# Routed experts' blocks add to two DRAM sums by turns instead of one

## The chip, the cores and the metric

The program runs on one core of a Trainium2 chip. The time is the device time of one execution in microseconds, given as the median of three runs. A profile of one execution shows when each engine worked: TensorE (PE, with its weight loads PEld apart), VectorE (DVE), ScalarE (ACT), GpSimd (POOL), and the queues from which transfers are issued (SP's, ACT's and POOL's).

## The reference

One layer: two token mixers, then a mixture of experts on 1024 tokens of width 1024. Only the second half bears on the change:

```
scores = sigmoid(xt @ router)                  # 64 experts, 8 chosen for every token
...
def expert_block(acc, blk):                    # 128 rows of one expert
    toks, wr, e = blk
    xb = x_pad[toks]
    hid = silu(xb @ w1[e]) * (xb @ w3[e])
    return acc.at[toks].add((hid @ w2[e]) * wr[:, None])
...
shared = (silu(xt @ ws1) * (xt @ ws3)) @ ws2
x = x + g2 * (acc[:n_tok] + shared)            # then the last norm
```

## The kernel before, in words

All products are made exact by splitting each fp32 operand into a high and a low part (`wh`, `wl` of weights, `xh`, `xl` of tokens), so one product takes three matmuls.

Ahead of the experts a projection stage turns the merged branches into the residual stream. It reads `mgd`, a DRAM tensor whose 16 parts POOL writes (L802) while TensorE still works on them, through SP's loads at L745, each waiting for `mgd`'s part. In the same stage a tile of zeros is made by POOL (L848) and written once by ACT's queue below the rows of the sum (L849), for rows of padding. The shared expert's output is then written into the sum `acc`, a DRAM tensor of 1024 + 128 rows (L979).

The routed experts (`moe`, L1535) run as a list of blocks of 128 rows, built on the chip: 95 blocks always, with further ones only if the list is longer. The list has two lanes, so that blocks b and b + 2 may share an expert. A block's weights are three pieces of 1 MB, loaded by SP (L1576) two blocks ahead; a piece is skipped where block b - 2 had the same expert. For block b, in the order written by hand in `group` (L1680 to L1706): POOL gathers the token rows of block b + 2 out of `h2d` into `xg`, which has two buffers (L1593); TensorE multiplies block b by the first two matrices (`up`, result `pa`); ACT scales the result of block b - 2 into `y`, which has two buffers (L1669), and POOL adds `y` to the rows of `acc` by an indirect transfer that reads, adds and writes (L1670); ACT and DVE split the weights of coming blocks (L1581, L1586); TensorE transposes the tokens of block b + 1 (`x_t`, L1603, result `pt`), then multiplies block b - 1 by its third matrix (`down`, result `py`). In what follows, "store" is the transfer at L1670 and "gather" the one at L1593. POOL's queue runs them in order, gather of b + 2, store of b - 2, gather of b + 3, and so on.

Each store adds to the tensor that the store before it adds to, so the framework makes POOL wait until the one before has landed.

The last stage (`final`, L1743) loads `acc` and the residual stream `x1d` in the order of rows, two transfers of 64 rows for each tile of 128 (L1740, on SP's queue), multiplies by the gate `g2` (L1777), adds the residual (on TensorE for tiles 0, 1, 3, 4, 6, on DVE at L1782 for the others), and norms and writes the output (L1789, L1790). All loads stand ahead of all output transfers on SP.

Of the kernel before, what the change touches and what calls it, by code (L numbers as in the profile page):

```python
# [10 lines left out]
F32 = mybir.dt.float32  # L11
# [28 lines left out]
def tile_kernel(ctx: ExitStack, tc: tile.TileContext, A: dict, dbg=None):  # L40
# [24 lines left out]
    acc = dram("acc", (T + P, D))  # L65
# [16 lines left out]
    def rsqrt(v, q):  # L82
        """1 / sqrt(v + EPS): the root's reciprocal, then one step of Newton's."""
        y, t = [q.tile([P, 4], F32, name=n, bufs=2)[:, : v.shape[1]] for n in ("rs_y", "rs_t")]
        S.activation(y, v, AF.Sqrt, bias=eps)
        V.reciprocal(y, y)
        V.scalar_tensor_tensor(t, v, EPS, y, ALU.add, ALU.mult)
        V.scalar_tensor_tensor(t, t, -0.5, y, ALU.mult, ALU.mult)
        V.scalar_tensor_tensor(y, t, 1.5, y, ALU.add, ALU.mult)
        return y  # L90
# [9 lines left out]
    def half(dt=F32):  # L100
        """Half of a row of x, or of the low part of h, which takes its place."""
        return hp.tile([P, 512], dt, name="xl", bufs=2 * KD)
# [60 lines left out]
    with tc.manual_schedule(), tc.tile_pool(name="stp", bufs=1, space=PSUM) as qp, ExitStack() as small:  # L163
# [5 lines left out]
        def load_wa(g, which=range(4)):  # L169
            # in the places of weights that come later  # L170
# [31 lines left out]
        # sums over partitions run in four column groups of the array at a time, and sel adds them up  # L202
# [50 lines left out]
        def stats(r):  # L253
            """One over the root of the mean square of each token, over all partitions."""
# [46 lines left out]
        def u_half(m, n, ps):  # L301
            for c in range(4):
                # token = ((c8, j), row); chunk of eight = row * 8 + c8
                dst = us[m][:, :, 32:160].rearrange("p j (r c) -> p c j r", c=8)[:, n * 4 + c]
                V.tensor_copy(dst, ps.rearrange("p (c j r) -> p c j r", c=4, j=8)[:, c])
# [101 lines left out]
    def values(h):  # L407
        """The values of a pair of heads, tokens in rows."""
# [27 lines left out]
    ones_b = ones[:, 0:1].broadcast_to([P, LC])  # L436
    with tc.tile_pool(name="gl", bufs=4, reuse_waits="tile") as q, \
# [9 lines left out]
        def keys(h, d, out):  # L447
            """Decays and keys of a head in one direction, and what the scores take of them."""
# [16 lines left out]
            # all that one table of functions serves, then all of the other's  # L465
# [17 lines left out]
            # the context's keys  # L483
# [48 lines left out]
        def attend(h, d, K, nK):  # L532
            """The head's output in one direction."""
# [15 lines left out]
            for n in order:  # L549
                ki, qi, qin, kp, d3, _ = K[n]  # L550
                # scores of 128 tokens: both chunks on the diagonal, then the block between them
# [68 lines left out]
        def finish():  # L620
            """The normed output, features in rows."""
# [43 lines left out]
    def gates(m):  # L665
        """The sigmoids of both branches' gates, for the features of tile m."""
# [29 lines left out]
    with tc.tile_pool(name="gl2", bufs=1, reuse_waits="tile") as q:  # L696
# [10 lines left out]
        def cmv(t):  # L707
            # (l, (row, c8)) read in the order of the tokens, (c8, l, row)
# [43 lines left out]
    with tc.tile_pool(name="mw", bufs=1, reuse_waits="tile") as qm, \  # L752
            tc.tile_pool(name="mgp", bufs=2, space=PSUM, reuse_waits="tile") as qp:
        wacc = qm.tile([P, D], F32, name="wacc")
        def mod_row(m):
            """Half of the sums behind a later modulation row; the row itself after the second."""
# [71 lines left out]
    def slot(tag, dt=F32R, n=D):  # L828
        """A tile in the place of one that this stage no longer needs."""
        return q.tile([P, n], dt, name=tag, tag=tag)  # L830

    with tc.tile_pool(name="woz", bufs=6, space=PSUM, reuse_waits="tile") as zp, \
# [16 lines left out]
        nc.scalar.dma_start(acc[T : T + P], zr)  # L849
# [8 lines left out]
        def proj(ts):  # L858
            """Sums of the projection's products for these tiles, eight features' tiles deep."""
# [11 lines left out]
        def norm2(t):  # L871
            """Residual, second norm, and the transposed halves of its result."""
# [26 lines left out]
        def scores(n):  # L899
            """The router's scores of half the tokens."""  # L900
# [18 lines left out]
        def shared_up(zp, n, m):  # L919
            """The shared expert's hidden features of tile m for half the tokens."""  # L920
# [37 lines left out]
    with tc.tile_pool(name="shz", bufs=4, space=PSUM, reuse_waits="tile") as zp:  # L958
# [8 lines left out]
        for t in range(8):  # L967
# [11 lines left out]
            nc.sync.dma_start(acc[ts], yo)  # L979
    xs_.close()  # L980
    if stop_after <= 6:
        dump("x1d", x1d)
        dump("h2d", h2d)
        dump("acc", acc)
# [7 lines left out]
    moe(nc, tc, A, ident, h2d, acc, gi, si, beb, iot, meta, lambda: final_load(nc, A, fin, x1d, modr))  # L992
    final(nc, tc, ident, fin, x1d, acc, A["out"])


def s5_main(nc, sp, pp, A, ud, kd, wtd, cad, phd, r8d, yd):
# [5 lines left out]
    for hh in range(2):  # L1002
# [5 lines left out]
        for d in range(2):  # L1008
# [18 lines left out]
            # out of the rotating frame, scan, and back  # L1027
# [56 lines left out]
def s5_tables(nc, tc, A, cad, phd, r8d, more, q, qt, par, bt, ct):  # L1084
# [3 lines left out]
    class Later:  # L1088
        """Keeps the calls of an engine for a chain of steps."""
# [9 lines left out]
    def chain():  # L1099
        """The calls kept so far, one at a time."""  # L1100
# [9 lines left out]
    def weave(*chains):  # L1110
        """Chains that don't wait for each other, by turns."""
# [30 lines left out]
    # sine and cosine of th: quarter turns taken off, then series  # L1142
# [36 lines left out]
    # cos - 1 without cancellation where no quarter turn came off  # L1179
# [4 lines left out]
    # exp(x) - 1: series near zero, the table elsewhere  # L1184
# [32 lines left out]
    def cmul_steps(or_, oi, ar_, ai, br, bi, shp, E=V, own=None):  # L1217
        """(or_ + i oi) = (ar_ + i ai)(br + i bi)."""
# [31 lines left out]
    # powers 0..8 of the decay, upwards and downwards  # L1250
# [18 lines left out]
    # the decay over eight tokens: modulus kept apart from the unit phase  # L1269
# [13 lines left out]
    # output matrices, the imaginary parts with the other sign  # L1283
# [7 lines left out]
    def phases(d, X):  # L1291
        """Unit phases of 0..159 groups of eight tokens."""
# [31 lines left out]
def s5_tables2(nc, tc, last, lastL, A, ident, kd, wtd, qp, q, qt, cmul, phases, bb, ca, pw, dn):  # L1324
    V, S, G, PE = nc.vector, nc.scalar, nc.gpsimd, nc.tensor
    # input matrices, transposed for the tensor engine
# [16 lines left out]
    if True:  # L1343
        # the kernel within eight tokens
        for b8 in range(2):
            kts = q.tile([P, 2560], F32, name=f"big{b8}")[:16, :1920].rearrange("c (g t) -> c g t", g=8)
            kv_ = kts.rearrange("c (i two) t -> c i two t", two=2)
            # each pair of a direction and a group's half in its own columns of the array
# [19 lines left out]
def dispatch(nc, tc, A, ident, ones, sc, gi, si, beb, iot, meta, h2d):  # L1368
    V, S, G, PE = nc.vector, nc.scalar, nc.gpsimd, nc.tensor
    with tc.tile_pool(name="ds", bufs=1, side="right", reuse_waits="tile") as q, \  # L1370
# [17 lines left out]
        # the two largest of every group, by merging sorted pairs  # L1388
# [17 lines left out]
        # a group's rank: how many are larger, or equal and before it  # L1406
# [20 lines left out]
        # weights  # L1427
# [8 lines left out]
        # places: tokens before this one with the same expert  # L1436
# [15 lines left out]
        # blocks of every expert  # L1452
# [17 lines left out]
        # number of blocks, and half of it rounded up: the list's two lanes  # L1470
# [21 lines left out]
        # the expert of every block  # L1492
# [23 lines left out]
        for i in range(0, 64, 4):  # L1516
            # rows and blocks of four choices at a time, the token's number carried by the block's side
# [17 lines left out]
def moe(nc, tc, A, ident, h2d, acc, gi, si, beb, iot, meta, later):  # L1535
    V, S, G, PE = nc.vector, nc.scalar, nc.gpsimd, nc.tensor
    with tc.tile_pool(name="mo", bufs=1, reuse_waits="tile") as q, tc.tile_pool(name="mop", bufs=1, space=PSUM, reuse_waits="tile") as qp:
# [16 lines left out]
        # in the order in which the stage before leaves its memory  # L1554
# [51 lines left out]
        def x_split(b):  # L1606
# [9 lines left out]
            # the token's weight for this block's expert  # L1616
# [49 lines left out]
        def store(b):  # L1666
            if b in YP:
                y = rot(q, [P, D], F32, "y", 2)
                S.mul(y, YP.pop(b), rw[:, b : b + 1])  # L1669
                G.indirect_dma_start(acc, IndirectOffsetOnAxis(ap=si[:, b : b + 1], axis=0), y, None,  # L1670
                                     compute_op=ALU.add)

        def group(lo, hi):
# [6 lines left out]
            for b in range(lo, hi):  # L1680
# [9 lines left out]
                if last:  # L1690
                    # no other block may follow
# [36 lines left out]
def final_load(nc, A, fin, x1d, modr):  # L1728
    """What the last stage needs and the experts' stage leaves room for."""
# [6 lines left out]
def by_row(nc, dst, src, t):  # L1736
    """Rows of 64 columns each, two to a tile, out of the order by columns."""
# [5 lines left out]
def final(nc, tc, ident, fin, x1d, acc, out):  # L1743
    V, S, G, PE = nc.vector, nc.scalar, nc.gpsimd, nc.tensor
    g2, fg = fin[:2]
    with tc.tile_pool(name="fi", bufs=1, reuse_waits="tile") as q, \
            tc.tile_pool(name="fip", bufs=4, space=PSUM, reuse_waits="tile") as qp:
        # the first memory that the experts' stage leaves
        n = len(fin) - 2
        xs = fin[2:] + [q.tile([P, D], F32, name=f"xx{t}") for t in range(n, 8)]  # L1750
        as_ = [q.tile([P, D], F32, name=f"a{t}") for t in range(8)]
        mh = q.tile([P, 1], F32, name="mh")
# [6 lines left out]
        def add(t, x, first):  # L1759
            """Adds x to the sum of a tile on the tensor engine."""  # L1760
# [5 lines left out]
        with tc.manual_schedule():  # L1766
            for t in range(-2, 8):
# [3 lines left out]
                if t >= 0:  # L1771
                    by_row(nc, as_[t], acc[0:T], t)
            for t in on_pe[:4]:
                add(t, xs[t], True)
            for t in range(10):
                if t < 8:
                    V.tensor_tensor(as_[t], as_[t], g2, ALU.mult)  # L1777
# [18 lines left out]
def prep(I):  # L1796
# [32 lines left out]
    # (kind, dir, pair, two, p) -> (two p), kind, (dir pair)  # L1829
# [20 lines left out]
    # constants of the shapes  # L1850
# [37 lines left out]
```

## Time and profile before

| What | Value |
|---|---|
| median of 3 runs | 2209.92 us (2206.99 to 2211.71) |
| span of the profiled execution, which is its own time | 2210.6 us |
| mean granted TensorE clock | 0.967 |
| busy: PE, DVE, ACT, POOL | 2055.3, 1548.2, 1216.4, 526.6 us |
| experts' stage: first token transpose to last `down` | 1174 to 2152 us |
| last stage: first load of the sum to the end | 2170.6 to 2210.6 us |

Busy time says which engine had instructions under way, not which one set the pace; matmuls overlap, so PE looks busier than it is. For the pace one looks at what ended each wait, stage by stage.

### The profile page before, as it was taken

The numbers are of one execution on the slowest core, as the hardware profiler recorded it, in microseconds if no ns is written. First come the engines' busy times: TensorE is split into PE (matmuls) and PEld (weight loads), VectorE is DVE, ScalarE is ACT, GpSimd is POOL, SyncE is SP. The second block draws the span as 40 slices with busy tenths as digits, with TensorE's granted clock in tenths as the row PEclk, the third lists the DMA queues.
The fourth block names the chain that finished last, engine by engine and source line by source line (L and its number), as shares of the span: only waits on it lengthen the run. The fifth ranks groups of instructions, "written<-read, shape, count | busy, mean of one in ns | idle before, by whom it ended". The sixth has DMA issues, their size and how long they took to land.

```text
span 2210.6 us, 28581 instructions
## 1 busy us (share of the span) xinstructions
PE 2055.3 (93%) x10575; PEld 1663.9 (75%) x10575; DVE 1548.2 (70%) x2168; ACT 1216.4 (55%) x1481; POOL 526.6 (24%) x386
## 2 busy tenths in 40 slices
PE   6799999999999999999999999999999998899994
PEld 2488888898777788877777877777777777677771
DVE  7855654744776643345688988988788887888874
ACT  4335543634533311122337887887787787777871
POOL 5510000000011000001003433344353333333342
PEclk7799999999999999999989999999999999999997
DMA  8150101111153543365327999888888889997968
GB/s 300 71 156 20 39 30 39 38 40 38 42 195 113 171 133 116 95 205 206 136 82 270 301 310 307 266 262 239 248 259 259 253 240 339 314 322 231 328 144 210
DMA packets 105210, 407.15 MB, mean 184 GB/s; under 512 B 14850, under 2 KB 21634, under 8 KB 85092
## 3 DMA queue, kind: packets, MB, share of 16 engines
q1 hardware_dynamic: 61408, 255.83, 33.2%
q0 software_dynamic: 34080, 130.93, 22.6%
q10 hardware_dynamic: 9572, 18.46, 2.3%
q8 instruction: 85, 1.39, 0.3%
q14 instruction: 65, 0.53, 0.1%
HBM read 461.24 MB, written 85.48 MB: 247 GB/s over the span
## 4 chain that ended last, share of the span: by engine, by line
PE 42%; DMA 32%; DVE 13%; ACT 5%; issue 5%; POOL 1%; SPq 1%; POOLq 0%; ACTq 0%; DVEq 0%
DMA acc<-y,si 24%; PE z L78 8%; PE z L79 8%; PE z L80 8%; DMA xg<-h2d,gi 3%; DVE wl L1586 3%; PE pa L1623 1%; PE pa L1624 1%; PE pa L1622 1%; ACT wh L1581 1%; PE pt L1603 1%; PE psc L555 1%; DVE xl L1614 1%; PE py L1622 1%; PE py L1623 1%
## 5 line engine op out<-in xcount | busy, mean ns | idle before, releaser
L1586 DVE TENSOR_TENSOR wl<-raw,wh 128x2048 fp32r<-128x2048 f32 x285 | 648.7, 2287 | 99.3 <-ACT wh L1581 99.2
L1581 ACT CAST wh<-raw 128x2048 fp32r<-128x2048 f32 x285 | 535.9, 1916 | 8.3 <-DMA raw<-in_wm_dram 8.3
L1670 POOL DMA_INDIRECT acc<-y,si x95 | 219.4, 2309 | 547.2 <-DMA acc<-y,si 245.9
L1622 PE MATMUL pa<-wh,xh 128*128 128x512 f32 x760 | 304.4, 401 | 0.2 <-ACT xh L1613 0.2
L1623 PE MATMUL pa<-wl,xh 128*128 128x512 f32 x760 | 298.0, 392 | 3.2 <-DVE wl L1586 3.2
L1624 PE MATMUL pa<-wh,xl 128*128 128x512 f32 x760 | 297.3, 391 | 0.1
L79 PE MATMUL z<-xl,wH 128*128 128x512 f32 x672 | 271.0, 403 | 9.0 <-DVE xl L291 9.0
L78 PE MATMUL z<-hH,wH 128*128 128x512 f32 x672 | 268.8, 400 | 2.7 <-ACT hH L288 1.6
L80 PE MATMUL z<-hH,wL 128*128 128x512 f32 x672 | 267.0, 397 | 0.0
L1593 POOL DMA_INDIRECT xg<-h2d,gi x97 | 162.5, 1675 | 91.6 <-issue 48.0
L1669 ACT ACTIVATE y<-py,rw 128x1024 f32<-128x1024 f32 x95 | 106.6, 1122 | 119.8 <-DMA acc<-y,si 119.5
L1623 PEld LDWEIGHTS pa<-wl,xh 128*128 128x128 f32 x760 | 143.0, 188 | 34.9 <-DVE wl L1586 7.9
L1624 PEld LDWEIGHTS pa<-wh,xl 128*128 128x128 f32 x760 | 142.7, 188 | 31.4 <-DVE xl L1614 1.6
L1622 PE MATMUL py<-wh,hh 128*128 128x512 f32 x380 | 163.3, 430 | 1.5 <-ACT y L1669 1.5
L1622 PEld LDWEIGHTS pa<-wh,xh 128*128 128x128 f32 x760 | 142.8, 188 | 27.1 <-ACT xh L1613 0.5
L123 DVE TENSOR_TENSOR wL<-wraw,wH 128x1024 fp32r<-128x1024 f32 x56 | 73.7, 1324 | 124.7 <-ACT wH L118 124.6
L1603 PE MATMUL pt<-ident,xg 128*128 128x128 f32 x760 | 105.9, 285 | 55.7 <-DMA xg<-h2d,gi 55.7
L79 PEld LDWEIGHTS z<-xl,wH 128*128 128x128 f32 x672 | 127.7, 190 | 35.5 <-DVE xl L291 12.5
L1623 PE MATMUL py<-wl,hh 128*128 128x512 f32 x380 | 154.3, 406 | 0.0
L1624 PE MATMUL py<-wh,hl 128*128 128x512 f32 x380 | 154.1, 405 | 0.0
L78 PEld LDWEIGHTS z<-hH,wH 128*128 128x128 f32 x672 | 127.6, 190 | 28.1 <-ACT hH L288 1.8
L1603 PEld LDWEIGHTS pt<-ident,xg 128*128 128x128 f32 x760 | 90.5, 146 | 76.8 <-DMA xg<-h2d,gi 68.5
(520 smaller groups left out, 3863.5 us busy)
## 6 DMA issues: line engine op xcount, KB each, us to landing
raw<-in_wm_dram SPq DMA_DIRECT2D x285, 1024.0 KB
wraw<-in_wz_dram SPq DMA_DIRECT2D x50, 512.0 KB
wk<-in_w_ada_dram SPq DMA_DIRECT2D x64, 256.0 KB
raw<-in_wm_dram POOLq DMA_DIRECT2D x6, 1024.0 KB, 7.4
xl<-in_xcT_dram SPq DMA_DIRECT2D x16, 256.0 KB
mgd<-ga POOLq DMA_DIRECT2D x16, 256.0 KB, 3.1
xr<-in_xc_dram SPq DMA_DIRECT2D x8, 512.0 KB
x1d<-xr ACTq DMA_DIRECT2D x8, 512.0 KB
```

The source lines that it names most:

```text
L78: PE.matmul(out, lh, rh, start=start, stop=False)
L79: PE.matmul(out, lh, rl, start=False, stop=False)
L80: return PE.matmul(out, ll, rh, start=False, stop=stop)
L1581: S.copy(WH[b, c], raw[b % 2][c])
L1586: V.tensor_tensor(WL[b, c], raw[b % 2][c], WH[b, c].bitcast(F32), ALU.subtract)
L1593: G.indirect_dma_start(XG[b], None, h2d, IndirectOffsetOnAxis(ap=gi[:, b : b + 1], axis=0))
L1603: PE.transpose(PX[b][hf][:, k * P : k * P + P], XG[b][:, (hf * 4 + k) * P : (hf * 4 + k + 1) * P], ident)
L1622: PE.matmul(out, lh, rh, start=start, stop=False)
L1623: PE.matmul(out, lh, rl, start=False, stop=False)
L1624: PE.matmul(out, ll, rh, start=False, stop=stop)
L1669: S.mul(y, YP.pop(b), rw[:, b : b + 1])
L1670: G.indirect_dma_start(acc, IndirectOffsetOnAxis(ap=si[:, b : b + 1], axis=0), y, None, compute_op=ALU.add)
```

## The change

There are two DRAM sums. `accs[0]` begins as the shared expert's output, as before; `accs[1]` begins at zero, written by nine transfers of POOL's queue out of the tile of zeros. Even blocks add to the first, odd ones to the second. The last stage loads both and adds them on DVE. (Comments that the change deletes are left out below; they move line numbers alone.)

```diff
-    acc = dram("acc", (T + P, D))
+    accs = [dram(f"acc{i}", (T + P, D)) for i in range(2)]
...
         G.memset(zr, 0.0)
-        nc.scalar.dma_start(acc[T : T + P], zr)
+        nc.scalar.dma_start(accs[0][T : T + P], zr)
+        for t in range(9):
+            nc.gpsimd.dma_start(accs[1][t * P : t * P + P], zr)
...
-            nc.sync.dma_start(acc[ts], yo)
+            nc.sync.dma_start(accs[0][ts], yo)
...
-                G.indirect_dma_start(acc, IndirectOffsetOnAxis(ap=si[:, b : b + 1], axis=0), y, None,
+                G.indirect_dma_start(accs[b % 2], IndirectOffsetOnAxis(ap=si[:, b : b + 1], axis=0), y, None,
                                      compute_op=ALU.add)
...
         as_ = [q.tile([P, D], F32, name=f"a{t}") for t in range(8)]
+        bs_ = [q.tile([P, D], F32, name=f"b{t}") for t in range(8)]
...
                 if t >= 0:
-                    by_row(nc, as_[t], acc[0:T], t)
+                    by_row(nc, bs_[t], accs[1][0:T], t)
+                    by_row(nc, as_[t], accs[0][0:T], t)
...
                 if t < 8:
+                    V.tensor_tensor(as_[t], as_[t], bs_[t], ALU.add)
                     V.tensor_tensor(as_[t], as_[t], g2, ALU.mult)
```

On POOL, at the beginning of the projection stage, the rows before are these (`x` is the tile of zeros, `ga` a finished part of the merged branches):

```order
L802 DMA mgd<-ga 128x4x128 x14
L848 MEMSET x_8153 128x1024
L802 DMA mgd<-ga 128x4x128 x2
L884 TENSOR_SCALAR ss<-ss 128x1
L885 TENSOR_TENSOR ss<-ss,mhalf 128x1
```

And after the change:

```order
L802 DMA mgd<-ga 128x4x128 x14
L848 MEMSET x_8153 128x1024
L852 DMA acc<-x_8153 128x1024 x4
L802 DMA mgd<-ga 128x4x128
L852 DMA acc<-x_8153 128x1024 x3
L802 DMA mgd<-ga 128x4x128
L852 DMA acc<-x_8153 128x1024 x2
L887 TENSOR_SCALAR ss<-ss 128x1
```

Four of the nine zero writes now stand ahead of the last-but-one write of `mgd`, seven ahead of the last. In the experts' stage the rows of POOL stand as before.

On SP, in the last stage, the rows before (`a` takes the sum, `xx` the residual):

```order
L1740 DMA xx_19063<-x1d 64x1024 x2
L1740 DMA a_19066<-acc 64x1024 x2
L1740 DMA a_19067<-acc 64x1024 x2
L1740 DMA a_19068<-acc 64x1024 x2
```

And after (`b` takes the second sum):

```order
L1744 DMA xx_19072<-x1d 64x1024 x2
L1744 DMA b_19083<-acc 64x1024 x2
L1744 DMA a_19075<-acc 64x1024 x2
L1744 DMA b_19084<-acc 64x1024 x2
L1744 DMA a_19076<-acc 64x1024 x2
L1744 DMA b_19085<-acc 64x1024 x2
L1744 DMA a_19077<-acc 64x1024 x2
```

Each of the eight tiles has two more loads, ahead of its old ones, and the outputs still stand behind all loads.

## Rows read from the trace of the kernel before

**Rows 1.** The page's chain that ended last, share of span by line.

```profile
DMA acc<-y,si 24%; PE z L78 8%; PE z L79 8%; PE z L80 8%; DMA xg<-h2d,gi 3%; DVE wl L1586 3%; PE pa L1623 1%; PE pa L1624 1%; PE pa L1622 1%; ACT wh L1581 1%; PE pt L1603 1%; PE psc L555 1%; DVE xl L1614 1%; PE py L1622 1%; PE py L1623 1%
```

**Rows 2.** Chain of waits, 1380 to 1480: start us, us, what.

```profile
1401.23 12.71 DMA acc<-y,si
...
1414.71 9.88 DMA acc<-y,si
```

**Rows 3.** What reads or writes `acc`, whole run: who waited (us, times); landing.

```profile
  POOL acc L1670: 245.9, 34
  ACT y L1669: 119.5, 54
...
DMA to landing us min/median/max: 6.0/9.4/14.6
```

**Rows 4.** POOL in order of time: start us, us, what, [idle before].

```profile
1225.75 2.05 POOL L1670 DMA_INDIRECT acc<-y,si  x1 [1.09 <-DMA acc<-y,si]
```

**Rows 5.** All engines in order of time, the end of the stores.

```profile
2151.66 0.39 PE L1624 MATMUL py<-wh,hl 128*128 128x512 f32 x1
2154.01 1.11 ACT L1669 ACTIVATE y<-py,rw 128x1024 f32<-128x1024 f32 x1 [5.04 <-DMA acc<-y,si]
...
2162.05 1.55 POOL L1670 DMA_INDIRECT acc<-y,si  x1 [5.81 <-DMA acc<-y,si]
```

**Rows 6.** PE in order of time, two token transposes running on.

```profile
1246.79 1.03 PE L1603 MATMUL pt<-ident,xg 128*128 128x128 f32 x8
...
1256.10 1.03 PE L1603 MATMUL pt<-ident,xg 128*128 128x128 f32 x8
```

**Rows 7.** PE in order of time, one that waits.

```profile
1348.29 1.09 PE L1603 MATMUL pt<-ident,xg 128*128 128x128 f32 x8 [3.65 <-DMA xg<-h2d,gi]
```

**Rows 8.** Stretches: L1603's PE, PEld busy (count), clock, DMA share, GB/s.

```profile
1174.00:1300.00 126.00, 14.40 (x112) 12.83 (x111) 1.00 0.90 287
1300.00:1500.00 200.00, 21.29 (x160) 18.03 (x160) 0.99 0.88 281
1500.00:1650.00 150.00, 16.84 (x112) 13.97 (x112) 0.97 0.88 253
1650.00:1800.00 150.00, 16.60 (x116) 14.43 (x117) 0.98 0.81 241
1800.00:2008.00 208.00, 22.08 (x152) 18.35 (x151) 0.95 0.94 315
2008.00:2152.00 144.00, 14.62 (x112) 12.64 (x111) 0.99 0.81 231
```

**Rows 9.** Groups by line, 1174 to 2152: busy, mean ns | idle before.

```profile
L1603 PE MATMUL pt<-ident,xg 128*128 128x128 f32 x760 | 105.9, 285 | 55.7 <-DMA xg<-h2d,gi 55.7
```

**Rows 10.** DMA queues, 1190 to 2160: packets, MB, share of 16 engines.

```profile
q1 hardware_dynamic: 22240, 158.35, 44.3%
q0 software_dynamic: 27035, 101.57, 42.7%
```

**Rows 11.** DMA queues, 2174 to 2192.

```profile
q1 hardware_dynamic: 1303, 4.26, 103.9%
```

**Rows 12.** All engines in order of time, last stage.

```profile
2180.79 5.98 SPq L1740 DMA_DIRECT2D a<-acc  x6
...
2187.47 16.94 SPq L1790 DMA_DIRECT2D out_dram<-a  x8
...
2190.80 1.23 DVE L1777 TENSOR_TENSOR a<-a,fin 128x1024 f32<-128x1024 f32 x1 [1.05 <-DMA a<-acc]
```

**Rows 13.** POOL in order of time, projection stage.

```profile
961.15 0.96 POOL L848 MEMSET x<- 128x1024 f32 x1 [17.10 <-PE z L80]
968.35 0.75 POOL L802 DMA_DIRECT2D mgd<-ga  x1 [6.24 <-DVE ga L801]
```

**Rows 14.** Stretches: PE, PEld, DVE, ACT, POOL busy, clock, DMA share, GB/s.

```profile
970.00:980.00 10.00, 5.75 (x23) 3.12 (x21) 5.11 (x6) 2.34 (x3) 0.75 (x1) 1.00 0.85 296
980.00:990.00 10.00, 8.88 (x32) 6.69 (x33) 3.59 (x3) 3.05 (x4) 0.00 (x0) 0.83 0.96 353
```

More of the change, by code (lines that the diff above doesn't have):

```diff
@@ L983, in tile_kernel @@
         dump("h2d", h2d)
-        dump("acc", acc)
+        dump("acc", accs[0])
         dump("sc", sc)
@@ L991, in tile_kernel @@
         return
-    moe(nc, tc, A, ident, h2d, acc, gi, si, beb, iot, meta, lambda: final_load(nc, A, fin, x1d, modr))
-    final(nc, tc, ident, fin, x1d, acc, A["out"])
+    moe(nc, tc, A, ident, h2d, accs, gi, si, beb, iot, meta, lambda: final_load(nc, A, fin, x1d, modr))
+    final(nc, tc, ident, fin, x1d, accs, A["out"])
 def s5_main(nc, sp, pp, A, ud, kd, wtd, cad, phd, r8d, yd):
@@ L1532, in dispatch, with moe @@
         V.tensor_tensor(si, t1, iv, ALU.add)
-def moe(nc, tc, A, ident, h2d, acc, gi, si, beb, iot, meta, later):
+def moe(nc, tc, A, ident, h2d, accs, gi, si, beb, iot, meta, later):
     V, S, G, PE = nc.vector, nc.scalar, nc.gpsimd, nc.tensor
@@ L1740, in by_row, with final @@
         nc.sync.dma_start(dst[r * 64 : r * 64 + 64], v[t * 2 + r])
-def final(nc, tc, ident, fin, x1d, acc, out):
+def final(nc, tc, ident, fin, x1d, accs, out):
     V, S, G, PE = nc.vector, nc.scalar, nc.gpsimd, nc.tensor
```

## The prediction

> **What bounds the kernel now.** I read the chain that ended last first. Nearly a quarter of the whole span in it is one thing: the landing of the experts' stores into `acc` [rows 1]. All of these lie between 1174 and 2170 us, so in that stage the stores hold about half of the time. The chain in order of time shows how: a store begins at 1401.23, lands 12.71 us later, at 1413.94, and the next begins at 1414.71; so 0.77 us lie between one landing and the next store [rows 2]. A store takes 6.0 to 14.6 us to land, 9.4 in the middle, and both POOL and ACT wait for it (245.9 us and, for a free `y` buffer, 119.5 us) [rows 3]. That the chain binds nearly throughout follows from two starts: the first store that waited for one before it starts at 1225.75 [rows 4], the last one at 2162.05 [rows 5]. Between them lie 91 steps in 936.3 us, 10.29 us each: the middle landing of 9.4 and 0.77, and little else.
>
> TensorE can do better. Where nothing holds it, two token transposes, which come once a block, start at 1246.79 and 1256.10: 9.31 us a block [rows 6]. What holds it is the gather, which stands behind the waiting store in POOL's queue: at 1348.29 a transpose waited 3.65 us for its rows [rows 7], and all such waits sum to 55.7 us over 95 blocks (760 transposes, eight a block) [rows 9]. The stage from 1174 to 2152 is 978 us; 95 blocks at 9.31 are 884. So something under 94 us is lost, 56 in waits, and part of the rest at a lower granted clock, 0.95 to 0.99 in the stretches with waits against 1.00 in the first [rows 8].
>
> Last I asked what stands behind the stores: the DMA engines. Their packets fill 44.3 + 42.7 = 87% of 970 us, the second queue being that of gathers and stores [rows 10]. By stretch the share is 0.81 to 0.94 [rows 8].
>
> **The change in the experts' stage.** No instruction is removed there. A store now waits for the one two blocks before. At 9.31 us a block that one was issued some 18.6 us earlier, more than the longest landing, 14.6 [rows 3]; so neither POOL nor ACT should wait for a landing, the gather is issued when its buffer is free, and the 9.31 us pace could hold until the DMA engines are full. The price of that second bound I take stretch by stretch [rows 8]: blocks are the count divided by 8, times 9.31 us for TensorE; the DMA work is the share times the length.
>
> - 1174 to 1300: 14 blocks, 130 us for TensorE: already at its pace, nothing to gain.
> - 1300 to 1500: 20 blocks, 186 us; DMA work 176.
> - 1500 to 1650: 14 blocks, 130 us; DMA work 132.
> - 1650 to 1800: 14.5 blocks, 135 us; DMA work 122.
> - 1800 to 2008: 19 blocks, 177 us; DMA work 196.
> - 2008 to 2152: 14 blocks, 130 us; DMA work 117.
>
> If the DMA engines could be filled wholly, each stretch would take the longer of its two numbers, and the gains are 14 + 18 + 15 + 12 + 14 = 73 us. If DMA were no bound, the gain would be at most what TensorE lost; 978 less 884, less some 8 us in which the last block runs out after its transpose, is 86. But weights come only two blocks ahead, and loads come in runs (experts with one block load every time), so a stretch can't level its work. The fullest stretch now reaches 0.94. With no stretch above 0.94, the five need 187, 140, 135, 208 and 130 us, and gain 13 + 10 + 15 + 0 + 14 = **51 us**, which I take. As the low end I take 25: half of it, if packets of stores, gathers and weights that now meet more often take longer each.
>
> Behind the last block: TensorE's last product ends at 2152.05, the last `y` begins at 2154.01, held by a landing, and takes 1.11 us, and the last store begins only at 2162.05, held by the store before it [rows 5]. Without either wait `y` is ready near 2153.2, and the store can begin some 8 us sooner than it did. It then shares the engines with the one before; I take **7 us** gained (0 to 8).
>
> **The last stage.** Sixteen more loads of 64 rows (256 KB each) go into SP's queue ahead of the outputs. Six loads of that form are issued in 5.98 us, from 2180.79 on, 1.1 us apart [rows 12], while the queue is full: 4.26 MB in 18 us at a share of 103.9%, 237 GB/s [rows 11]. Sixteen cost 17.7 us by that rate. They lie on the path, since a multiply at 2190.80 still waits for its load and the outputs are issued behind all loads [rows 12]. The eight adds on DVE, 1.23 us each by the multiply of the same shape [rows 12], fall into the time in which DVE waits for loads: a tile's four loads now take 4.4 us, and its two to three operations with the final one under 5. Only the last tile's add is bare. Against that, DVE is behind the loads today: the multiply at 2190.80 is that of the sixth tile, two more follow, and the last output is issued 13.6 us later (16.94 us of issuing from 2187.47) [rows 12]. With loads slower than DVE one tile is left when the last load is in, which I estimate at 10 us for its four operations on DVE and its square and root. That gives back some 4 of the 17.7: **+14 us** (10 to 18).
>
> **The zero writes.** Nine transfers of 512 KB, 4.7 MB, behind the memset that ends at 962.1 on POOL [rows 13]. Four stand ahead of the write of `mgd` at 968.35, three more ahead of the last one, in the same queue; the loads of the next products wait for that first write. The four (2.1 MB) have 6 us before it, and at the 296 GB/s of the next stretch they need 7, so the write is late by a few us at most. The other 2.6 MB meet loads that fill the engines to 0.85 and 0.96 in 970 to 990, while TensorE is idle for 5.4 of those 20 us and waits for them [rows 14]. At 353 GB/s they are 7.4 us of DMA; if half comes ahead of loads that TensorE waits for, 3.7. With the delay of the write I take **+5 us**. The low end is 0 (all fits into the slack of single loads), the high end 14, all 4.7 MB at 324 GB/s, the mean of the two stretches, on the path. POOL's next work, the small norms, comes some 40 us later and doesn't feel it.
>
> **Sum.** 2210.6 - 51 - 7 + 14 + 5 = 2171.6 in terms of the span of the profiled execution. The median of the runs shown is 0.7 us less: **2171 us**.
>
> **Rivals.** *DMA is the bound (slower).* The place is the experts' stage: 855 us of DMA work, the sum of shares times lengths, in 978 us [rows 8]. Nothing is taken from it, and it is pressed together. If packets then take 12% longer, 958 us, the stage gains 20 and loses most of it again to the late stage and zero writes; at 15%, 983 us, it gains nothing, and the time is 2210.6 - 7 + 14 + 5 - 0.7 = 2222. The point that decides is a stage that gains less than 12 us. For it speaks the dense stretch, at 0.94 already; against it, that the first stretch runs at 9.31 us a block with a share of 0.90. The Trainium skill's DMA: Bandwidth & Descriptors, section Issuing engines are not separate DMA queues, says the same thing as a rule: transfers started from any engine run on the same 16 engines and interleave, so more of them in flight adds no bandwidth. The dense stretch agrees with that rule; the other four, with shares of 0.81 to 0.90, leave room that a rule on bandwidth doesn't speak of.
>
> *The whole loss comes back.* DMA levels itself out, as in the first stretch, and the pace is 9.31 to the end: 2210.6 - 86 - 8 + 14 + 5 - 0.7 = 2135. The dense stretch speaks against it.
>
> *The edges cost more.* The zero writes lie on the path in full (14) and the last stage's loads too (18): 2210.6 - 51 - 7 + 18 + 14 - 0.7 = 2184. The idle TensorE at 970 to 990 speaks for it.
>
> **How the numbers follow.** Chances: the forecast 0.60, DMA as the bound 0.14, the whole loss back 0.13, dear edges 0.13. A difference of 0.2%, 4.4 us, is about what a measurement of this kernel can tell from no change. Forecast, second and third rival all end faster; of the first, a small part does (stage gains of 16 to 25). So faster 0.87, same 0.05, slower 0.08. The likeliest case alone runs from 2146 to 2190 (a gain of 25 to 73 in the stage with the other terms at their middle). The range goes down to the whole loss back, 2135, and up to a stage gain of about 9 us, 2206.
>
> **What would show it.** Right: in the profile after, stores no longer start 0.77 us behind a landing but behind their `y`; ACT's wait for landings is gone; transposes wait little for gathers; waits for weights (ACT's split for `raw`) appear in the dense part, with DMA shares near 0.94 and above; the last stage is 14 us longer, with loads at the old rate; the first products after 970 start a few us later. Wrong: store landings of 15 us and more, so that they bind again; or DMA shares above 0.95 throughout with a pace of still over 10 us a block.

## The result, and the profile after

The changed kernel takes 2170.49 us (median of 4 runs, 2167.81 to 2172.61), the kernel before on the same chip 2208.45; the ratio is 0.9835, with an interval of 0.9813 to 0.9857. The forecast was 2171. The number came out right, its terms less so. The two profiled executions, one of each program, can be cut at five events that both have: the memset ahead of the zero writes, the first token transpose, the end of the last product, the first load of a sum, the end of the span.

| us | before | after | difference | predicted |
|---|---|---|---|---|
| start to the memset | 961.15 | 965.37 | +4.2 | 0 |
| memset to first transpose | 212.8 | 223.3 | +10.5 | +5 (zero writes) |
| first transpose to end of last product | 978.1 | 913.4 | -64.7 | -51 (stage) |
| to the first load of a sum | 18.6 | 10.1 | -8.5 | -7 (tail) |
| to the end | 40.0 | 57.5 | +17.5 | +14 (last stage) |
| span | 2210.6 | 2169.7 | -40.9 | -39 |

The page's chain that ended last, by engine and by line, no longer has a row of stores as [rows 1] had; TensorE is the chain, and the one DMA of weight in it is the weights' load:

```profile
PE 69%; DMA 11%; DVE 11%; ACT 5%; issue 3%; SPq 1%; POOL 0%; DVEq 0%; ACTq 0%; POOLq 0%
PE z L78 9%; PE z L79 9%; PE z L80 9%; PE pa L1626 6%; PE pa L1627 6%; PE pa L1625 6%; DMA raw<-in_wm_dram 5%; PE py L1626 3%; PE py L1627 3%; PE py L1625 3%; PE pt L1606 3%; DVE wl L1589 2%; DMA xg<-h2d,gi 1%; DMA a<-acc 1%; PE psc L555 1%
```

POOL in order of time, two gathers and two stores. A store starts 0.30 us behind the gather, not behind a landing as in [rows 4], and the pairs come 9.31 us apart:

```profile
1227.80 2.32 POOL L1596 DMA_INDIRECT xg<-h2d,gi  x1 [3.45 <-issue]
1230.43 2.84 POOL L1674 DMA_INDIRECT acc<-y,si  x1 [0.30 <-issue]
1237.11 2.31 POOL L1596 DMA_INDIRECT xg<-h2d,gi  x1 [3.85 <-issue]
1239.73 2.83 POOL L1674 DMA_INDIRECT acc<-y,si  x1 [0.30 <-issue]
```

The view of all tiles named `acc`, 1160 to 2140 (what the stores waited for; the landing times). The two waits of [rows 3], 245.9 and 119.5 us, are gone (one wait of 3.2 us at a gather is all that is still put down to a landing), although a store takes longer to land than before, 12.0 us in the middle:

```profile
its engine sat idle before it (us, times) until:
  issue: 26.2, 86
  ACT y L1672: 20.0, 8
...
DMA to landing us min/median/max: 6.4/12.0/14.4
```

The waits in the same stretch (who waited for what: us, times, longest). In place of the stores stand the weights: ACT waits 44.4 us for them, and TensorE feels a part of it, in the `y` and the hidden features `hd` that ACT and VectorE then make late:

```profile
ACT wh L1584 <- DMA raw<-in_wm_dram: 44.4, 33, 11.1
...
POOL acc L1674 <- ACT y L1672: 20.0, 8, 10.5
...
PE py L1625 <- ACT y L1672: 7.2, 2, 5.8
PE ph L1648 <- DVE hd L1641: 6.9, 7, 1.2
```

The stage in stretches, cut at the first transposes of the same blocks (14, 20, 14, 15, 18, 14 blocks; the columns are those of [rows 8]; the DMA share sums the times of packets and can pass 1 by a little):

```profile
1188.65:1317.39 128.74, 14.49 (x113) 13.05 (x113) 1.00 0.90 285
1317.39:1507.35 189.96, 20.68 (x161) 18.63 (x161) 1.00 0.94 307
1507.35:1647.29 139.94, 14.47 (x112) 13.04 (x112) 0.98 0.88 260
1647.29:1786.89 139.60, 15.51 (x120) 13.97 (x120) 1.00 0.91 268
1786.89:1962.23 175.34, 18.62 (x144) 16.78 (x144) 1.00 1.02 353
1962.23:2102.04 139.81, 14.48 (x112) 12.90 (x111) 1.00 0.84 245
```

In the kernel before the same blocks took 128.7, 207.5, 146.7, 152.1, 199.0 and 144.1 us, so the gains are 0, 17.5, 6.8, 12.5, 23.7 and 4.3. The dense stretch, forecast at no gain, gained most, and its granted clock rose from 0.95 to 1.00; before, it looked like this:

```profile
1808.97:2007.96 198.99, 21.35 (x144) 17.71 (x144) 0.95 0.95 321
```

The projection stage, against [rows 14] (PE, PEld, DVE, ACT, POOL, clock, DMA share, GB/s). The DMA engines are full for 30 us, TensorE is idle for 12.7 of these, and its granted clock falls behind the waits:

```profile
970.00:980.00 10.00, 7.14 (x32) 4.88 (x30) 4.65 (x7) 0.00 (x0) 4.16 (x7) 0.98 0.98 340
980.00:990.00 10.00, 5.99 (x18) 4.21 (x18) 3.68 (x3) 4.02 (x4) 0.00 (x0) 0.68 1.01 386
990.00:1000.00 10.00, 4.17 (x10) 3.31 (x11) 4.45 (x4) 4.15 (x5) 0.00 (x0) 0.67 0.98 373
```

The last stage: from 2122.68 on, two loads of 64 rows take 2.2 us, the old rate of 1.1 us each, and the outputs begin behind them:

```profile
2143.51 1.56 SPq L1744 DMA_DIRECT2D b<-acc  x2
2145.79 1.46 SPq L1744 DMA_DIRECT2D a<-acc  x2
2147.95 15.61 SPq L1797 DMA_DIRECT2D out_dram<-a  x8
```

### The profile page after: what moved, and what is told of

The parts are those of the page before. It is cut to its first block, busy times and chain, and to the rows that moved or that the text cites. A ratio compares the mean times of both kernels' runs of the same rounds, so it can differ in the third digit from the quotient of the medians.

```text
span 2169.7 us, 28631 instructions
## 1 busy us (share of the span) xinstructions
PE 2041.0 (94%) x10575; PEld 1658.1 (76%) x10575; DVE 1560.2 (72%) x2176; ACT 1222.6 (56%) x1481; POOL 647.2 (30%) x395
## 3 DMA queue, kind: packets, MB, share of 16 engines
q0 software_dynamic: 35376, 135.65, 23.7%
## 4 chain that ended last, share of the span: by engine, by line
PE 69%; DMA 11%; DVE 11%; ACT 5%; issue 3%; SPq 1%; POOL 0%; DVEq 0%; ACTq 0%; POOLq 0%
PE z L78 9%; PE z L79 9%; PE z L80 9%; PE pa L1626 6%; PE pa L1627 6%; PE pa L1625 6%; DMA raw<-in_wm_dram 5%; PE py L1626 3%; PE py L1627 3%; PE py L1625 3%; PE pt L1606 3%; DVE wl L1589 2%; DMA xg<-h2d,gi 1%; DMA a<-acc 1%; PE psc L555 1%
## 5 line engine op out<-in xcount | busy, mean ns | idle before, releaser
L1589 DVE TENSOR_TENSOR wl<-raw,wh 128x2048 fp32r<-128x2048 f32 x285 | 644.4, 2286 | 11.0 <-ACT wh L1584 11.0
L1584 ACT CAST wh<-raw 128x2048 fp32r<-128x2048 f32 x285 | 537.8, 1920 | 44.5 <-DMA raw<-in_wm_dram 44.4
L1596 POOL DMA_INDIRECT xg<-h2d,gi x97 | 222.0, 2289 | 415.1 <-issue 327.3
L1674 POOL DMA_INDIRECT acc<-y,si x95 | 267.6, 2817 | 46.5 <-issue 26.2
L1625 PE MATMUL py<-wh,hh 128*128 128x512 f32 x380 | 157.1, 413 | 7.2 <-ACT y L1672 7.2
L79 PEld LDWEIGHTS z<-xl,wH 128*128 128x128 f32 x672 | 127.8, 190 | 34.9 <-DVE xl L291 11.7
L1626 PE MATMUL py<-wl,hh 128*128 128x512 f32 x380 | 149.5, 393 | 0.8 <-DVE wl L1589 0.8
L1627 PE MATMUL py<-wh,hl 128*128 128x512 f32 x380 | 149.4, 393 | 0.0
L80 PEld LDWEIGHTS z<-hH,wL 128*128 128x128 f32 x672 | 128.2, 191 | 24.6 <-issue 0.7
L118 ACT CAST wH<-wraw 128x1024 fp32r<-128x1024 f32 x56 | 58.8, 1050 | 149.2 <-PE z L79 66.0
L613 POOL TENSOR_SCALAR ss<-ss 128x4 f32<-128x4 f32 x12 | 4.4, 366 | 440.3 <-DVE ss L612 440.3
```

The costliest lines, as they stand in the source:

```text
L79: PE.matmul(out, lh, rl, start=False, stop=False)
L80: return PE.matmul(out, ll, rh, start=False, stop=stop)
L1584: S.copy(WH[b, c], raw[b % 2][c])
L1589: V.tensor_tensor(WL[b, c], raw[b % 2][c], WH[b, c].bitcast(F32), ALU.subtract)
L1596: G.indirect_dma_start(XG[b], None, h2d, IndirectOffsetOnAxis(ap=gi[:, b : b + 1], axis=0))
L1625: PE.matmul(out, lh, rh, start=start, stop=False)
```

## The experiments

The theory is that of the prediction: the gain is the store chain alone, the weights are what is left of it, and the edges are paid for in DMA. Ratios are to the kernel before on the same chip. "The stage" is first transpose to end of last product.

**one_chain: the edges without the second chain.**

```diff
-                G.indirect_dma_start(accs[b % 2], ...
+                G.indirect_dma_start(accs[0], ...
```

> The changed kernel with all stores into the first sum again; zero writes and the added loads of the last stage stay. Theory (the whole gain is that a store no longer waits for the one before it): the store chain is back at about 10.3 us a step and the edges stay, so 2208 for the kernel before, plus 9 for the zero writes and 17 for the last stage: 2234 (2226 to 2242), waits of POOL for a landing near 246 us again. Rival (the gain comes from other places in memory or another order of the program): it stays below 2200.

Ratio 1.0116 (1.0073 to 1.0158), some 25 us slower (16 to 35), 2235.62 us. The stage is 978.7 us, as before (978.1); POOL waits 251.0 us for landings and ACT 133.5. Everything that the change gained in the stage hangs on the store's target, and the edges cost some 25 us on their own (26.6 between the spans of the two profiled executions, 2237.2 and 2210.6).

**gather_early: one sum, gathers a block sooner.**

```diff
-            XG[b] = rot(q, [P, D + 64], F32, "xg", 2)
+            XG[b] = rot(q, [P, D + 64], F32, "xg", 3)
...
-                hh = rot(q, [P, 256], F32R, "hh", 2)
-                hl = rot(q, [P, 256], F32R, "hl", 2)
+                hh = rot(q, [P, 256], F32R, "hh", 1)
+                hl = rot(q, [P, 256], F32R, "hl", 1)
...
-                gather(b + 2)
+                gather(b + 3)
...
```

> The kernel before, one sum, with the gathers issued a block earlier into three buffers (and the split halves of the hidden features in one buffer each, which makes room). Theory (the rate of the store chain is the bound, about 10.3 us a step): the waits of transposes for gathers, 55.7 us, shrink by more than half, but the stage is as long as before and the wait goes to the free buffer of the output (ACT) instead; time 2200 to 2210. Rival (what costs is only that the gather stands behind a waiting store in POOL's queue): most of the 55.7 us come back, 2155 to 2175, like the changed kernel without its edges.

Ratio 0.9984 (0.9961 to 1.0007): no difference. The transposes' wait of 55.7 us [rows 9] is 0.0, and the time isn't back: ACT's wait for a free `y` grew from 119.5 to 169.8 us. In the view of the tiles `acc`:

```profile
who waited for it (us, times):
  POOL acc L1670: 238.3, 36
  ACT y L1669: 169.8, 68
```

The gather's wait was mostly a symptom: TensorE waits 34.5 us for the hidden features `hd` instead, where it had waited 0.6. The single buffers of `hh` and `hl` cost nothing that shows; ACT's waits ahead of `hh` are for its input, 13.2 us (46.8 before). In the one profiled execution the stage is 966 us, so at most 12 of the 55.7 us were the gather's own.

**no_weights: what the rest is.**

```diff
-            if b >= NB:
+            if b >= 2:
                 return
```

> The changed kernel without the loads of weights from the third block on (left out: those blocks compute with the weights of the first two). Theory (what is left above 9.31 us a block, some 23 us, is waits for weights on full DMA engines): ACT's waits for weights, 44 us, are gone, the pace is 9.31 throughout, the stage from first transpose to last product is 94 x 9.31 + 17 = 892 us instead of 913, and the time some 2149 (2143 to 2155). Rival (the rest is the stores and gathers themselves, or waits among the compute engines): the stage stays above 905 and the time above 2160.

2144.62 us in one run; the stage took 890.6 us, with a DMA share of 0.58, and ACT's wait for weights is gone:

```profile
1183.00:2074.00 891.00, 886.90 (x4373) 737.12 (x4371) 841.00 (x856) 782.67 (x758) 486.37 (x189) 1.00 0.58 121
```

So 23 of the changed kernel's 913 us are waits for weights; where no weights share the DMA engines with them, stores and gathers cost nothing any more.

**late_zero, after_again, mid_zero: the price of the zero writes.** First they were moved to a tile that I took to be free in the shared expert's stage:

```diff
-        for t in range(9):
-            nc.gpsimd.dma_start(accs[1][t * P : t * P + P], zr)
...
         fin = [fp.tile([P, D], F32, name=f"fin{i}") for i in range(6)]
+        G.memset(fin[0], 0.0)
+        for t in range(9):
+            nc.gpsimd.dma_start(accs[1][t * P : t * P + P], fin[0])
```

> The changed kernel with the nine zero writes moved out of the projection stage into the shared expert's stage, where the DMA share is 0.17 to 0.39, from a tile that stands empty there. Theory (the zero writes cost some 9 us because they stand ahead of loads that TensorE waits for): 2170.5 - 9 = 2161 (2158 to 2165), and the products after 970 start as early as in the kernel before, apart from a shift that comes ahead of the zero writes. Rival (they cost the same wherever they lie, since POOL's queue and the DMA engines are needed there too): within 3 us of the changed kernel, 2168 to 2173, with a later first block instead.

A miss: ratio 0.9865 (0.9836 to 0.9894), no faster than the changed kernel. The tile came free only behind the lists' work on VectorE, so that its memset starts at 1157.88. The nine writes then stood ahead of the first weights and gathers in POOL's queue, and the first transpose waited:

```profile
1192.54 1.94 PE L1607 MATMUL pt<-ident,xg 128*128 128x128 f32 x8 [17.28 <-DMA xg<-h2d,gi]
```

The place was wrong, and the time alone says nothing about the price; the trace of the projection stage does (below). In the second try the zeros come from a tile that the projections leave at 1076:

```diff
-        for t in range(9):
-            nc.gpsimd.dma_start(accs[1][t * P : t * P + P], zr)
...
+        z2 = slot("mL3", F32)
+        G.memset(z2, 0.0)
+        for t in range(9):
+            nc.gpsimd.dma_start(accs[1][t * P : t * P + P], z2)
         dispatch(nc, tc, A, ident, ones, sc, gi,
```

> The changed kernel once more, on the chip of the three runs beside it. Theory (the 4.2 us by which its profiled execution was late already at 135 us, ahead of every changed instruction, is a difference between executions): the shift is gone or other here, and the projections are late by the zero writes' 9 us alone; ratio near 0.9835 again. Rival (the shift belongs to the changed program): 4 us late at 135 us again.

> The changed kernel with the nine zero writes moved to the stretch behind the last projections (about 1085 to 1120 in its trace, DMA share 0.14 to 0.85, TensorE never idle), well ahead of the first weights of the experts. Theory (the zero writes cost 9 us only where TensorE waits for loads, and in late_zero they met the first weights and gathers): 9 us faster than the changed kernel (6 to 11), first block as early as in the kernel before. Rival (they cost wherever they lie): within 3 us of the changed kernel.

after_again: 2168.22 us, ratio 0.9821 (0.9791 to 0.9851). Its memset starts at 960.29, so the 4.2 us ahead of the zero writes belong to the one execution (in these kernels that memset starts anywhere from 956.25 to 965.37). From memset to first transpose it takes 222.0 us, again 9 more than before. mid_zero: 2154.82 us, ratio 0.9772 (0.9739 to 0.9804), and 211.1 us from memset to first transpose. So the zero writes cost 9 to 11 us in their first place. The first 45 us from the memset on show where, in the kernel before, after_again, late_zero and mid_zero (columns as in [rows 14]):

```profile
961.15:1006.15 45.00, 39.64 (x165) 30.47 (x164) 20.20 (x22) 12.31 (x13) 2.46 (x3) 0.96 0.70 246
960.29:1005.29 45.00, 33.99 (x124) 25.69 (x123) 19.23 (x22) 12.51 (x13) 7.27 (x12) 0.81 0.93 328
962.32:1007.32 45.00, 39.60 (x165) 30.95 (x164) 20.14 (x22) 12.31 (x13) 2.46 (x3) 0.96 0.70 245
956.96:1001.96 45.00, 41.37 (x163) 32.16 (x162) 20.25 (x22) 12.32 (x13) 2.46 (x3) 0.89 0.69 245
```

The count behind PE's busy time is that of its matmuls. With the writes elsewhere TensorE does as many here as in the kernel before (165 and 163 against 165); with the writes here it does 124, for it waits for loads and runs at a lower granted clock. So late_zero had this time back, and lost it again at the first gathers.

**first_only: the price of the second sum's loads.**

```diff
-                    by_row(nc, bs_[t], accs[1][0:T], t)
...
-                    V.tensor_tensor(as_[t], as_[t], bs_[t], ALU.add)
```

> The changed kernel whose last stage loads the first sum only and doesn't add the second (left out: half of the experts' results). Theory (the last stage's sixteen loads and eight adds cost 17.5 us on the path, all of it by the loads' own rate of 1.1 us each): 17 us faster than the changed kernel (15 to 19). Rival (part of what that stage takes longer is that the loads meet the last two stores): 10 to 14 us.

Ratio 0.9748 (0.9710 to 0.9787), 2150.38 us, 17.8 less than after_again beside it; from first load to the end 40.3 us, as before (40.0). The loads, with the adds behind them, are paid for in full.

**fold: a try to be rid of both edges.**

```diff
-    accs = [dram(f"acc{i}", (T + P, D)) for i in range(2)]
+    accs = [dram("acc", (T + P, D)), x1d]
...
                 S.mul(y, YP.pop(b), rw[:, b : b + 1])
+                G.tensor_tensor(y, y, g2, ALU.mult)
...
```

> Two sums without either edge: the second sum begins as the residual row x1, which is in memory already, and not at zero; the experts' outputs and the shared expert's are multiplied by the last modulation row before they are added (on POOL, and on VectorE for the shared expert), so that the last stage only loads and adds both sums, on TensorE. No zero writes, 32 loads of 64 rows in the last stage instead of 40 (24 before), three buffers for the output. Theory (the stage's gain of some 65 us is kept, the zero writes' 9 and half of the last stage's 17.5 come back, and POOL's multiply of some 2 us is hidden in its 45% idle time): 17 to 22 us faster than the changed kernel, 2148 to 2153 where that has 2170. Rival (POOL, whose gathers and stores already take 5.1 of 9.31 us, becomes the bound or delays gathers): the pace goes over 9.6 us a block and it is no faster than the changed kernel.

Ratio 1.0625 (1.0593 to 1.0657), 2345.86 us: no faster, as the rival had it, but by another mechanism. POOL is not full; VectorE is, at 250 of 250 us in a stretch, and TensorE waits 126 us for its split of the weights. That takes 3257 ns in the mean, 2286 in the changed kernel (1250 to 2200, VectorE by line):

```profile
L1586 DVE TENSOR_TENSOR wl<-raw,wh 128x2048 fp32r<-128x2048 f32 x247 | 798.1, 3257 | 0.0
```

The mean mixes two sorts. In order of time (VectorE, then POOL), a split is as short as before unless POOL multiplies beside it:

```profile
1521.73 2.28 DVE L1586 TENSOR_TENSOR wl<-raw,wh 128x2048 fp32r<-128x2048 f32 x1
1524.27 5.20 DVE L1586 TENSOR_TENSOR wl<-raw,wh 128x2048 fp32r<-128x2048 f32 x1
```
```profile
1524.90 2.40 POOL L1670 TENSOR_TENSOR y<-y,fin 128x1024 f32<-128x1024 f32 x1
```

So it goes in every block: two of its three splits take 2.28 us, and the one that has the multiply inside it takes 2.9 us longer, more than the multiply itself. The Trainium skill's GPSIMD Engine Reference, section Specifications, says that GpSimd's SBUF interfaces are shared with VectorE, with contention where VectorE reads two SBUF inputs; the split does, and the trace agrees (5.20 against 2.28 us).

**plain_rows: why a load of 64 rows takes 1.1 us.**

```diff
-                if t >= 0:
-                    by_row(nc, bs_[t], accs[1][0:T], t)
-                    by_row(nc, as_[t], accs[0][0:T], t)
+            for t in range(8):
+                for r in range(2):
+                    nc.sync.dma_start(bs_[t][r * 64 : r * 64 + 64], accs[1][t * P + r * 64 : t * P + r * 64 + 64])
+            for t in range(8):
+                nc.sync.dma_start(as_[t], accs[0][t * P : t * P + P])
```

> The changed kernel whose last stage loads rows of the sums as they lie in memory, without the change from columns to rows (left out: the order of the tokens in the sums): first the second sum in sixteen loads of 64 rows, then the first in eight loads of 128 rows. It measures what sets the 1.1 us of such a load. Theory A (the packets of 4 KB, or the 64 rows: a load of 64 rows is slow wherever the rows lie): the sixteen loads still go at about 237 GB/s, 17.7 us. Theory B (the rows lie 64 KB apart in memory, sixteen rows of 4 KB, and that slows their packets): well above 300 GB/s, under 14 us, and the eight loads of 128 rows go as fast.

Theory A in one half: it is the 64 rows, not their places, and not the packets of 4 KB, which both forms have. (2180.72 us in one run, with every load of the second sum ahead of the first's; the time says nothing here.) In turn the loads of 64 rows and of 128 rows, both with full engines:

```profile
2112.00:2128.00 16.00, 1.85 (x4) 0.55 (x4) 0.00 (x0) 0.00 (x0) 0.00 (x0) 0.72 1.04 234
2136.00:2140.00 4.00, 0.00 (x0) 0.00 (x0) 2.10 (x2) 0.00 (x0) 0.00 (x0) 0.50 1.02 393
```

Nor is it the size: in the changed kernel's first stage eight loads of 256 KB each, 128 rows of 2 KB, run as fast:

```profile
44.00:47.00 3.00, 2.96 (x16) 2.18 (x20) 0.71 (x3) 0.86 (x2) 2.92 (x5) 0.50 1.05 399
```

The Trainium skill's DMA: Bandwidth & Descriptors, section Rules for kernel authors, says that two transfers to disjoint halves of the partitions serialize, and that one of 128 partitions should be used; the trace agrees that one is better, 393 GB/s against 234.

**wide and best: a use of it.** Every eighth row of a sum makes a tile that one load of 128 rows can fetch; its tokens come back into order in the output's write.

```diff
-    for r in range(2):
-        nc.sync.dma_start(dst[r * 64 : r * 64 + 64], v[t * 2 + r])
+    nc.sync.dma_start(dst, src.rearrange("(p e) d -> e p d", e=8)[t])
...
-                    nc.sync.dma_start(out[0, w * P : w * P + P], as_[w])
+                    for j in range(2):
+                        r = j * 512 + w * 64
+                        nc.sync.dma_start(out[0, r : r + 64], as_[w][j : P : 2])
```

> The changed kernel whose last stage, and the four tiles loaded ahead of it, take every eighth row of the sums and of x1 in one load of 128 rows (512 KB), and write each output tile in two transfers of 64 rows from every other partition. Theory (a load of 128 rows goes at about 397 GB/s, 1.3 us, where two of 64 rows take 2.2 us, so the 20 tiles of the stage need 26 us instead of 44; then VectorE's 27 operations of 1.23 us, 33 us, are what the stage waits for): 8 us faster than the changed kernel (5 to 12). Rival (VectorE keeps up with the loads): all of the 17 us.

> The edit of mid_zero and that of wide together. Theory (they lie in different stages and add up): 2155 - 8 = 2147 where the changed kernel has 2169, ratio to the kernel before 0.973. Rival (the two edits disturb each other, or the one of wide gains nothing): ratio 0.977 as mid_zero alone.

wide: ratio 0.9779 (0.9732 to 0.9826), 2154.14 us; from the first load of a sum to the end 45.8 us instead of 57.5, so 11.7 of the 17.5 are back, at the upper end of what was expected. best: 0.9700 (0.9665 to 0.9735), 2137.32 us; the expected ratio, 0.973, lies inside that interval. The last stage now waits for VectorE, as the theory had it; of 35 us near the end of best (the span ends at 2135.2) it is busy for 32.6:

```profile
2096.00:2106.00 10.00, 5.38 (x8) 2.08 (x8) 9.07 (x8) 2.97 (x5) 2.17 (x4) 0.83 1.02 412
2106.00:2118.00 12.00, 5.95 (x12) 2.03 (x12) 11.86 (x11) 2.80 (x7) 4.69 (x7) 1.00 1.03 410
2118.00:2131.00 13.00, 3.78 (x4) 1.18 (x4) 11.63 (x10) 3.04 (x6) 4.86 (x7) 0.55 0.48 189
```

**best_spread: one block of 19 us.** In the changed kernel the longest wait for weights, 11.15 us, stands behind the ten loads for the last stage that SP issues at block 40 (SP's queue, then ACT):

```profile
1569.32 9.11 SPq L1744 DMA_DIRECT2D fin<-x1d  x8
```
```profile
1594.66 1.90 ACT L1584 CAST wh<-raw 128x2048 fp32r<-128x2048 f32 x1 [11.15 <-DMA raw<-in_wm_dram]
```

```diff
-                if b == 40:
-                    later()
+                if 25 <= b <= 40 and b % 3 == 1:
+                    later((b - 25) // 3)
...
```

> The kernel best, in which the six tiles that the last stage needs and that are loaded ahead of it, all at block 40, are loaded one every three blocks, from block 25 to 40. In the changed kernel ACT waits 11.15 us for weights just behind those loads, and one block takes 18.96 us there; in best 14.6 us. Theory (the weights are late because these loads stand ahead of them in SP's queue and fill the DMA engines): that block goes back to 9.31 us, and the kernel is 5 us faster than best (3 to 6), 2132. Rival (a run of blocks that all load weights is the cause, and the loads are not): the wait stays, or comes at another block, and the time is that of best within 2 us, 2137.

2130.26 us, ratio 0.9673 (0.9645 to 0.9701), the lowest time of all and 7 us under that of best, which was measured apart; the intervals of the two ratios overlap, so the times alone don't show the gain. The traces do for one execution each: the stage takes 904.3 us, in best 909.2. The block takes 9.31 us, and no wait of ACT for weights from 1290 to 2075 is longer than 2.9 (6.8 in best). Their sum didn't shrink, 41.4 us against 39.7 in best; what went is the one long wait:

```profile
ACT wh L1586 <- DMA raw<-in_wm_dram: 41.4, 37, 2.9
```

## Why the prediction was right, and where its steps were not

- **The chain of stores bound the stage**: right. one_chain brings it back whole, and the changed kernel has neither the stores' nor ACT's wait for a landing. That the gather holds TensorE was half right: its wait was the one that TensorE felt, but gather_early shows it to be a symptom. And a store that is free seldom waits for its `y` (8 times of 95); it mostly starts behind the gather ahead of it in POOL's queue. Landings grew from 9.4 to 12.0 us in the middle and stayed under 18.6, the distance of two blocks, as the step needed.
- **The stage, -51**: the mechanism was right and the term mis-sized; it measured -64.7 (-62.4 in after_again). The step that failed is "no stretch above 0.94". It took the fullest share of a stretch with waits in it for a limit. Freed of the chain, the dense stretch ran at 1.02 and 353 GB/s, and gained 23.7 us where 0 stood; it moved nearly the bytes of before (62 and 64 MB, rate times length), and its DMA work, share times length, was 179 us where it had been 189. The other stretches gained 41 where 51 stood: the one from 2008 was to take 130 us, and the last block's run-out of 8, which the bound of 86 had taken off, was left out there.
- **Weights are the next wait**: right. no_weights takes 22.8 us off the stage. Some 10 of these are the one block behind the preloads, 18.96 us instead of 9.31, a place that the prediction had not seen.
- **The tail, -7**: -8.5, right.
- **The last stage, +14**: +17.5. The place and, nearly, the old rate were right: from the first load of a sum to the first output SP takes 35.8 us instead of 16.8, 18.9 more. Of the 4 us to be given back, because VectorE was behind the loads, 1.4 came: from the first output to the end it is 21.7 us instead of 23.1. first_only's 17.8 is the same net price.
- **The zero writes, +5**: 9 to 11. The half that was to pass unnoticed did not; 12.7 us of idle TensorE in 970 to 1000 stand against 5.4 in 970 to 990 before, and the lower clock behind it.
- **The rivals.** *DMA is the bound* was wrong: DMA work did not grow dearer as the stage was pressed together. The section of the Trainium skill's DMA: Bandwidth & Descriptors that was cited for it, Issuing engines are not separate DMA queues, says that starting transfers from several engines saves only the time of issuing. The runs don't contradict that; the engines had room where the stores waited, and the dense stretch went from a share of 0.95 to 1.02. *The whole loss comes back* came three quarters of the way, 65 of 86. *The edges cost more* came nearly whole, 28 of 32.
- **The number**: that 2171 was met so closely is luck. The stage and the tail gained 15 us more than forecast, the edges cost 9 more, and 4.2 came from a shift of the one execution.
- **The range**: two of its figures don't follow from the prediction's own sum. Gains of 25 and 73 us in the stage give 2197 and 2149, not 2190 and 2146; and 2206 belongs to a gain of some 16 us, where 9 gives 2213.

## What to carry to other kernels

Where a chain of read-modify-write stores sets the pace, a second target frees it, and what it frees is to be read per stretch; a DMA share of 0.94 with waits in the stretch is no ceiling. The price lies at the edges: filling and reading the second target are plain DMA, so put the filling where TensorE does not wait for loads, check when the memory that it uses comes free, and read with all 128 partitions. Before work is moved to POOL, check what VectorE does beside it. Once a big wait is gone, look along every queue for what it had covered, such as a batch of preloads.

## What the runs showed of the hardware

- Loads of 64 rows run at 234 GB/s with the DMA engines full, loads of 128 rows at 393, for rows of 4 KB in both (plain_rows); 128 rows of 2 KB, no larger a load than the slow ones, go at 399, and 64 rows that lie 64 KB apart at the same 235 to 237.
- VectorE's two-input operation on 128x2048 takes 2.28 us, and 5.20 with a POOL multiply of 2.40 us inside it; beside POOL's gathers and stores it stays at 2.28 (fold).
- Landings of accumulating stores grew to 12.0 us in the middle with two chains, and no store waited for one; with one chain they were 9.4 and set the pace.
